# Loaded operands of 256-column matmuls begin 52 bytes behind their stream modulo 256, not 88

## The chip, the cores and the metric

One Trainium2 chip, one of its cores. The metric is the device time of one execution in microseconds; of the kernel before three runs are shown, and their median is 273.35 us (273.21 to 273.37).

## What is computed

One decoder layer on 256 tokens of width 1024, in float32. A hybrid mixer projects x with one combined matrix (1024 x 5120), makes an attention group, a gated linear recurrence (RG-LRU) and a gated short convolution of it, and projects their concatenation back (1536 x 1024); a layer norm follows, then cross-attention with 4 heads into 256 memory tokens, and a second layer norm. Cut to what matters:

```python
proj = x @ w_in                                  # (256, 1024) @ (1024, 5120)
q, k, v, g_att, x_lru, g_lru, sc_b, sc_c, sc_x, g_sc = split(proj, 10)
y = stack([moba_attention(q, k, v), rg_lru(causal_dwconv(x_lru)), sc_b * causal_dwconv(sc_c * sc_x)])
x = layer_norm(ALPHA * x + (group_rms_norm(y) * silu(gates)) @ w_out)
q, k, v = x @ wq, mem @ wk, mem @ wv             # 4 heads of 256
x = layer_norm(ALPHA * x + softmax(q @ k.T / 16) @ v @ wo)
```

## The kernel before

Every large product is made of three float32r products: each operand is split into a high part (an ACT copy, line 88) and a low part (a DVE subtraction, line 89), and TensorE adds high x high, high x low and low x high in one bank. The weights come in 42 chunks of 128 x 2048 numbers; `ORDER` (lines 40 to 55) is their order. SP loads a chunk into one of three `raw` buffers, ACT and DVE split it in two pieces into `whi` and `wlo` (four buffers each, pool `splp`), and TensorE reads these. The order of TensorE's work is that of the program, with small steps moved between the matmuls by the planner of the framework; chunks are split up to two ahead of the one in use.

TensorE takes two operands from SBUF in a matmul: one is loaded into the array ahead of time (a weight load, PEld in the profile), and the other streams through it. Each weight load here has 128 columns, 512 bytes in a partition, and the load for the next matmul goes on while the present one streams. There are two kinds of chunk:

- "Transposed" chunks (fourth entry of `ORDER` true; `proj_t`, lines 121 to 135): the weights are loaded and the activations stream, 256 columns or 1024 bytes each. These are the 16 chunks of the q, k, short-convolution and gate projections (the last two on tiles named `scc`, `scx`, `scb`, `gate`), the four of the cross-attention's keys (`km`) and the four of its queries (`xq`), 48 matmuls each. The first projection (`xlru`, line 194) works the same way with 96 matmuls.
- The others (`mm_n`, lines 140 to 148): the activations are loaded and the weights stream, 512 columns each, for the attention's values (`vb`), the mixer's output (`op`) and the memory's values (`vm`). The last projection (`ob`) uses this helper with 256 columns.

Where the operands begin in SBUF is set by hand. `at` (lines 70 to 76) gives a tile LINE = 64 numbers (256 bytes) more than it needs and returns it from a given number on. Weights that are loaded begin at AT_LOAD = 22 numbers (88 bytes), weights that stream in 512 columns at AT_STREAM = 7 (28 bytes), those of the last projection at 0. The buffers themselves begin at a multiple of 256 bytes, or 128 bytes past one (pool `con`, which holds x, the memory and their split parts; for tiles that meet these, HALF = 32 numbers is added). So in all 256-column matmuls of float32r numbers the loaded operand lies 88 bytes behind the streamed one modulo 256: the projections, the small gates of the recurrence (`early`, lines 270 to 289), the cross-attention's scores (`xs`, queries at HALF + AT_LOAD against keys at HALF) and values (`xo`), and `ob` (`oh` and `ol` at HALF + AT_LOAD). They are 24 x 48 + 96 + 24 + 48 + 48 + 192 = 1560 matmuls of about 2000. In the 512-column ones it is 228 bytes (`vb`, `vm`) or 100 (`op`). All later steps in a chunk are multiples of 256 bytes, so the difference stays through a chunk.

Of the kernel before, what the change touches and what calls it, by code (L numbers as in the profile page):

```python
# [26 lines left out]
XW = S + G  # L27


AT_LOAD, AT_STREAM, LINE, HALF = 22, 7, 64, 32  # L30
RAW, SPL, PIECES = 3, 4, 2


# [687 lines left out]
```

## Time and profile before

| | us |
|---|---|
| median of three runs | 273.35 |
| the profiled execution | 273.52 |
| its span, first to last instruction | 271.7 |
| PE busy in the span | 262.6 |
| DVE busy | 203.6 |
| ACT busy | 153.7 |

The profile has a page of sums and a trace that can be asked for more. PE is TensorE's matmuls, PEld its weight loads. The chain is the work that ended last, followed back from the end; its rows merge neighbours of one line and tile, so that time divided by count is the distance from one matmul's start to the next one's (the pitch). In a timeline row the second number is from the first start to the last end of the merged instructions, so a pitch is read there as the distance between starts of two rows, divided by the matmuls between them.

### The profile page before, as it was taken

To read this page: it belongs to the slowest core of one execution; us is meant where nothing else is said; L and a number is where in the kernel's file an instruction comes from. 1 tells how busy PE (TensorE), PEld (TensorE's weight loads), DVE (VectorE), ACT (ScalarE), POOL (GpSimd) and SP (SyncE) were. 2 spreads that over 40 slices of the span, in tenths; PEclk is the share of its full clock that TensorE was granted. 3 is DMA by queue.
4 is the path that set the end of the run, shared out by engine and by line. 5 is a ranking of instruction groups with operands and counts; after the bars stand their busy time and mean duration, and the time that the engine had idled before them with its cause. 6 is when DMAs were issued, how large, how long until landed. Compare 5 with 4: busy or idle time off the path is not lost.

```text
span 271.7 us, 4877 instructions
## 1 busy us (share of the span) xinstructions
PE 262.6 (97%) x2003; PEld 246.7 (91%) x2003; DVE 203.6 (75%) x279; ACT 153.7 (57%) x239; POOL 48.4 (18%) x67
## 2 busy tenths in 40 slices
PE   8999999999999999999999999999999999999990
PEld 5899998799999999999888889998899998899990
DVE  3889956699886998886897689957464759733735
ACT  4779599955995455746842344336554628623000
POOL 5582003006360979100000000000000000000000
PEclk9999999999999999999999999999999999999997
DMA  6994797244408647856675454687464440000012
GB/s 233 385 373 175 283 382 260 122 154 157 154 2 349 273 154 288 310 178 217 247 230 236 174 189 154 256 308 271 124 230 154 157 154 0 4 0 2 2 75 77
DMA packets 8118, 50.93 MB, mean 187 GB/s; under 512 B 912, under 2 KB 1312, under 8 KB 2464
## 3 DMA queue, kind: packets, MB, share of 16 engines
q1 hardware_dynamic: 8064, 50.60, 50.6%
q8 instruction: 15, 0.25, 0.3%
q14 instruction: 7, 0.06, 0.1%
q0 software_dynamic: 32, 0.03, 0.0%
HBM read 49.57 MB, written 1.05 MB: 186 GB/s over the span
## 4 chain that ended last, share of the span: by engine, by line
PE 92%; DMA 3%; DVE 2%; SPq 1%; ACT 1%; issue 0%; DVEq 0%
PE op L146 12%; PE gate L131 12%; PE vm L146 8%; PE xq L131 8%; PE ob L146 8%; PE km L131 8%; PE scb L131 4%; PE scc L131 4%; PE scx L131 4%; PE q L131 4%; PE vb L146 4%; PE k L131 4%; DMA raw_xw<-in_first 3%; PE xo L622 2%; PE xs L592 2%; PE xlru L194 2%
## 5 line engine op out<-in xcount | busy, mean ns | idle before, releaser
L89 DVE TENSOR_TENSOR wlo<-raw_w,whi 128x1024 fp32r<-128x1024 f32 x80 | 102.3, 1312 | 17.6 <-ACT whi L88 17.3
L88 ACT ACTIVATE whi<-raw_w 128x1024 fp32r<-128x1024 f32 x80 | 80.1, 1054 | 51.3 <-PE op L146 16.3
L146 PE MATMUL op<-whi,yh 128*128 128x512 f32 x64 | 16.7, 393 | 0.0
L146 PEld LDWEIGHTS op<-whi,yh 128*128 128x128 f32 x64 | 12.0, 189 | 2.6
L146 PE MATMUL op<-wlo,yh 128*128 128x512 f32 x48 | 13.0, 391 | 0.0
L131 PE MATMUL gate<-xh,wlo 128*128 128x256 f32 x96 | 12.8, 276 | 0.0
L131 PE MATMUL gate<-xh,whi 128*128 128x256 f32 x96 | 12.8, 276 | 0.0
L131 PE MATMUL gate<-xl,whi 128*128 128x256 f32 x96 | 12.8, 276 | 0.0
L501 DVE SCALAR_TENSOR_TENSOR xa<-op,rms,xa 128x512 f32<-128x512 f32 x12 | 8.8, 746 | 5.0 <-PE op L146 5.0
L131 PEld LDWEIGHTS gate<-xh,wlo 128*128 128x128 f32 x96 | 11.8, 188 | 0.0
L131 PEld LDWEIGHTS gate<-xh,whi 128*128 128x128 f32 x96 | 11.8, 188 | 0.0
L131 PEld LDWEIGHTS gate<-xl,whi 128*128 128x128 f32 x96 | 11.8, 188 | 0.0
L146 PEld LDWEIGHTS op<-wlo,yh 128*128 128x128 f32 x48 | 9.1, 189 | 2.0
L519 ACT ACTIVATE mvb<-mvb,eps_ln 128x1 f32<-128x1 f32 x2 | 0.6, 294 | 18.1 <-DVE mvb L518 18.1
L146 PE MATMUL ob<-whi,kml 128*128 128x256 f32 x64 | 10.2, 276 | 0.0
L146 PE MATMUL ob<-whi,kmh 128*128 128x256 f32 x64 | 10.1, 277 | 0.0
L146 PE MATMUL ob<-wlo,kmh 128*128 128x256 f32 x64 | 10.0, 276 | 0.0
L650 DVE SCALAR_TENSOR_TENSOR xa<-xa,ob 128x256 f32<-128x256 f32 (+1 forms) x7 | 3.2, 459 | 8.6 <-PE ob L146 8.4
L88 ACT ACTIVATE yh<-sg 128x512 fp32r<-128x512 f32 x6 | 3.8, 630 | 10.2 <-DVE sg L468 10.2
L131 PE MATMUL xq<-x1h,whi 128*128 128x256 f32 x64 | 9.3, 279 | 0.0
L146 PE MATMUL vm<-whi,mh 128*128 128x512 f32 x32 | 9.1, 399 | 0.0
L131 PE MATMUL xq<-x1l,whi 128*128 128x256 f32 x64 | 8.9, 277 | 0.0
(217 smaller groups left out, 638.0 us busy)
## 6 DMA issues: line engine op xcount, KB each, us to landing
raw_w<-in_w SPq DMA_DIRECT2D x40, 1024.0 KB, 4.8
lnv<-in_ln SPq DMA_DIRECT2D x2, 1024.0 KB, 8.1
raw_xw<-in_first SPq DMA_DIRECT2D x2, 768.0 KB, 8.4
xa<-in_x SPq DMA_DIRECT2D x1, 1024.0 KB, 6.8
raw_mem<-in_memt SPq DMA_DIRECT2D x1, 1024.0 KB, 4.8
raw_xw<-in_first SPq DMA_DIRECT2D x2, 384.0 KB, 6.1
raw_xw<-in_first SPq DMA_DIRECT2D x1, 512.0 KB, 4.1
out<-xa SPq DMA_DIRECT2D x2, 256.0 KB, 2.0
```

Of the source, the lines that this page charges most:

```text
L88: nc.scalar.activation(hi, src, AF.Copy)
L89: nc.vector.tensor_tensor(lo, src, hi.bitcast(F32), op=ALU.subtract)
L131: nc.tensor.matmul(ps[:, c], w[:, k, cs], a[:, k], start=n == 0, stop=n == 3 * KC - 1)
L146: nc.tensor.matmul(out, a[:, k0 + k, t * P:(t + 1) * P], part[w][:, k, c:c + out.shape[-1]], start=first and n == 0, stop=last and n == 11)
L194: nc.tensor.matmul(xlp[ct], w[:, k % 4, ct * P:(ct + 1) * P], x[:, k], start=k == 0 and m == 0, stop=k == 7 and m == 2)
L501: nc.vector.scalar_tensor_tensor(a, bk[t], rms[:, g, t:t + 1], a, op0=ALU.mult, op1=ALU.add)
L519: nc.scalar.activation(mv[:, 2:3], mv[:, 1:2], AF.Sqrt, bias=eps_ln)
L592: nc.tensor.matmul(ps[:, t], q[:, d, t * P:(t + 1) * P], k[:, 2 * h + d], start=n == 0, stop=n == 5)
L622: nc.tensor.matmul(po[:, d], v[:, m, c:c + P], p[:, m], start=n == 0, stop=n == 5)
L650: nc.vector.scalar_tensor_tensor(a, a, ALPHA, bank[:, :w], op0=ALU.mult, op1=ALU.add)
```

## The change

AT_LOAD, the place where loaded operands begin in their tiles, goes from 22 numbers to 13, from 88 bytes to 52. It is used for the transposed chunks and the first two (line 82), for the split gate weights of the recurrence (line 272), for `oh` and `ol` (line 509), for the memory's values `vmh` and `vml` (line 510) and for the queries `qh` and `ql` (line 582). No tile changes its size or its place, and no instruction, wait or transfer is added, removed or moved.

```diff
-AT_LOAD, AT_STREAM, LINE, HALF = 22, 7, 64, 32
+AT_LOAD, AT_STREAM, LINE, HALF = 13, 7, 64, 32
```

## Rows read from the trace of the kernel before

**Rows 1.** The page: busy time of TensorE's two parts, its granted clock in 40 slices.

```profile
PE 262.6 (97%) x2003; PEld 246.7 (91%) x2003; DVE 203.6 (75%) x279; ACT 153.7 (57%) x239; POOL 48.4 (18%) x67
PEclk9999999999999999999999999999999999999997
```

**Rows 2.** Chain that ended last, in order of time: start us, us, engine, tile, line.

```profile
13.25 4.93 PE xlru L194 x40
18.18 7.93 PE q L131 x68
...
43.06 11.04 PE vb L146 x48
...
62.72 5.60 PE scx L131 x48
...
96.23 32.64 PE gate L131 x288
...
129.16 33.24 PE op L146 x144
162.40 21.79 PE km L131 x192
184.19 1.75 PE x1t L548 x16
...
245.49 19.08 PE ob L146 x168
264.57 0.02 issue
264.59 0.43 DVE xa L650
```

**Rows 3.** Timeline of PE, ends of three long stretches: start us, us, instruction.

```profile
13.82 0.63 PE L194 MATMUL xlru<-xh,whi 128*128 128x256 f32 x4
...
27.82 0.28 PE L289 MATMUL gate<-xch,early 128*128 128x256 f32 x1
...
57.89 1.10 PE L131 MATMUL scc<-xl,whi 128*128 128x256 f32 x8
...
73.76 0.30 PE L331 MATMUL ss<-ones,thirds 128*128 128x1 bf16 x6
...
82.98 1.09 PE L131 MATMUL scx<-xl,whi 128*128 128x256 f32 x8
...
86.71 1.09 PE L131 MATMUL scx<-xh,wlo 128*128 128x256 f32 x8
...
217.25 1.09 PE L131 MATMUL xq<-x1l,whi 128*128 128x256 f32 x8
...
219.11 0.40 PE L592 MATMUL xs<-kmh,qh 128*128 128x256 f32 x2
```

**Rows 4.** Busy time by window: us, PE, PEld, DVE, ACT, POOL, PEclk, DMA share, GB/s.

```profile
57.89:72.82 14.93, 14.93 (x130) 14.93 (x129) 13.96 (x24) 9.79 (x28) 6.01 (x9) 1.00 0.37 123
82.98:86.71 3.73, 3.73 (x34) 3.73 (x33) 2.77 (x3) 1.09 (x3) 0.00 (x0) 1.00 0.97 406
75.76:79.39 3.63, 3.63 (x34) 3.63 (x33) 3.40 (x4) 3.63 (x6) 3.63 (x2) 1.00 0.02 5
96.06:127.80 31.74, 31.74 (x283) 31.74 (x281) 26.96 (x32) 18.75 (x24) 11.58 (x13) 1.00 0.65 235
```

**Rows 5.** Timeline of PE where `xo` and `ob` alternate: ends of 13 matmuls.

```profile
242.42 0.40 PE L622 MATMUL xo<-ptl,vmh 128*128 128x256 f32 x2
...
243.97 0.39 PE L622 MATMUL xo<-pth,vmh 128*128 128x256 f32 x2
```

**Rows 6.** DVE on `wlo`, 145 to 160 us (begins at 88), then 120 to 141 (28).

```profile
L89 DVE TENSOR_TENSOR wlo<-raw_w,whi x6: 1206/1216/1219, 146.5 to 159.3; 128x1024 fp32r<-128x1024 f32 x6
...
L89 DVE TENSOR_TENSOR wlo<-raw_w,whi x8: 1217/1222/1227, 119.1 to 138.7; 128x1024 fp32r<-128x1024 f32 x8
```

**Rows 7.** Waits: who waited for whom, us in total, times, longest.

```profile
ACT whi L88 <- PE scx L131: 2.8, 1, 2.8
```

## Prediction

> **What bounds the kernel now.** I read the busy times first: PE is busy for 262.6 of 271.7 us, and its granted clock is full in every slice but the last [rows 1], which is the level of 2.4 GHz. Next the chain in order of time, to see whether that busy time is also the path: from 13.25 to 264.57 us it is TensorE alone, matmul behind matmul [rows 2]. DVE takes over at 264.59 for the last layer norm, and ahead of 13.25 stand the first loads and splits. So each nanosecond of a matmul's pitch between those two times is a nanosecond of the kernel.
>
> Then I read the pitch, as time by count. One stretch of the chain has 288 matmuls of 256 columns in 32.64 us: 113.3 ns, which is 272 cycles at 2.4 GHz. Another has 48 of the same shape and the same offset in 5.60 us, which is 116.7 ns or 280 cycles; a third 68 in 7.93 us, 116.6 ns [rows 2]. So at one and the same offset there are two steady pitches, 3.33 ns or 8 cycles apart. The timeline shows long unbroken stretches at the slower one: 120 matmuls from 13.82 to 27.82 us (14.00 us, 116.7 ns each), 136 from 57.89 to 73.76 (15.87 us, 116.7 ns), 32 from 82.98 to 86.71 (3.73 us, 116.6 ns) and 16 from 217.25 to 219.11 (1.86 us, 116.3 ns) [rows 3].
>
> What picks the pitch is not another engine or the transfers. Two windows at 116.7 ns have a DMA share of 0.37 and of 0.97, two at 113.3 ns of 0.02 and of 0.65; POOL is busy throughout the window at 75.76 (113.3 ns) and idle throughout that at 82.98 (116.6 ns) [rows 4]. The pitch changes where the row of like matmuls is broken: behind the small gates, transposes or sums of another shape. I take it that each start sets how the weight load lies against the stream that runs beside it, that this repeats from matmul to matmul, and that the offset between the two operands says which repeating patterns there are. Behind a break the pitch can also be worse for a while: 13 matmuls where `xo` and `ob` alternate take 1.55 us, 119.2 ns each [rows 5].
>
> **The change, part by part.** It moves the start of the loaded operands, and that is all: nothing is issued, waited for or moved past a queue. There are three things to cost.
>
> *The writes of the splits.* ACT and DVE write the parts at another start. DVE's pieces take 1216 ns in the median where the tile begins at 88 bytes, and 1222 ns where it begins at 28 [rows 6], so the start does not show there. I cost it at nothing; what hides a few nanoseconds more is that the splits run ahead of TensorE.
>
> *Matmuls at 116.7 ns now.* Taken from the timeline in the way of [rows 3], 304 stand in the rows, and the like groups beside them (the rest of the `scc` and `scx` chunks, a few of `xq`) bring them to about 330. At the faster pitch they give back 330 x 3.33 ns = 1.10 us. Of the rest of the 1560, about 60 lie ahead of 13.82 us, most of them where splits set the time, some 110 are in the short transients behind breaks (at about 4 ns over 113.3 each, an estimate from the rows at 116 and 119 ns: 0.4 us in all), and about 1060 run at 113.3 ns, of which 648 stand in three rows of the chain (gate 288, km 192 at 113.5, ob 168 at 113.6 ns) [rows 2].
>
> *The price at 52 bytes.* No row has this offset with a long stretch, so it is bounded from both sides. From below: 113.3 ns is the least pitch in any stretch of 256 columns here. It is 17/16 of a cycle for each column, and by that same figure a matmul of 512 columns would take 226.7 ns; those of `vb` (at 228 bytes) take 11.04 us / 48 = 230.0 ns and those of `op` (at 100) 33.24 / 144 = 230.8 with their restart [rows 2]. No offset in this trace beats 17/16, so I take it as the floor. A lower end is the 109.4 ns of the 128-column transposes (1.75 us / 16) [rows 2], which load as many columns each: 3.9 ns less for 1500 matmuls. From above: the slower pitch, 116.7 ns, or far out the 119.2 of a transient [rows 5].
>
> I take the floor, since it is the value nearest to most rows: of the long stretches, some 1060 matmuls are on it and 330 are not, and a move by 36 bytes does away with the particular pattern that holds these 330. The sum: 273.52 us of the profiled execution less 1.10 is 272.42, and as that execution is 0.17 us above the median of the runs, 272.25 against 273.35; I say 272.2. The transients stay at their 0.4 us, because the breaks stay. What comes next behind a faster TensorE: in the window of the `scc`, `scx` and `scb` chunks DVE is busy for 13.96 of 14.93 us [rows 4], so its splits have 6% to spare for 3% of speed. One ACT split there waits 2.8 us for TensorE to free its buffer [rows 7]; such a wait shrinks as TensorE gets ahead. At the end nothing else is late before 264.57 us. If the cover fails in that stretch, half of its 0.45 us is lost.
>
> **A rule that speaks against it.** The two pitches at one offset, with all other engines different or idle, are what I have on how load and stream act on each other [rows 2 to 4]. The Trainium skill (SBUF — State Buffer, "Who interferes with whom") gives TensorE two independent read ports, one for the moving operand and one for weight loads, and says that it never waits on anyone; by that rule the offset is of no account and the time stays at 273.35 us. The trace neither proves nor excludes it, since it has no two long stretches that differ in the offset alone; it stands below as a rival. The skill's page on TensorE (TensorE: Matmul & The Clock Gate, "Wait — 56ns, not 53.3ns?") gives a warm gap of N/2.4 + 2.5 ns, 109.2 for 256 columns; the rows here have 113.3 and 116.7 instead.
>
> **The rivals.**
>
> *It settles on 280 cycles.* At 52 bytes the repeating pattern with 8 cycles more may be the one that holds everywhere. What speaks for it: the 288 matmuls of 512 columns pay 3.3 ns over 17/16 throughout [rows 2], and their offsets, 228 and 100, leave 4 modulo 16 as 52 does, while 88 leaves 8. If a fine position like that decides, the whole kernel goes to 116.7 ns. Against it: those have another length and another stream. Its price: 1060 x 3.33 = 3.53 us, 276.9. If each stretch falls to either pitch by chance, half of 1390 matmuls are at 116.7 ns instead of 330: 365 x 3.33 = 1.2 us more, 274.6. It decides from the point at which more than 330 of these 1390 run at 280 cycles.
>
> *Nothing that counts.* The pattern is set by how the queue restarts after a break, not by where the operands lie, or the offset doesn't bear on the load's reads at all, so that the change does not do what its words say. For it: both pitches exist at 88. Against it: the pitch holds for a hundred matmuls on end, which looks like a position that repeats. The time: 273.35, within 0.5.
>
> *Below the floor.* At 52 bytes load and stream don't meet, and the pitch comes down to the 109.4 ns of the transposes: 1500 x 3.9 = 5.9 us, and 1.5 for what now lies above 113.3 ns, 266. Against it: no full-rate stretch is under 17/16, at three offsets and two lengths.
>
> *Above 280 cycles.* All at the transient's 119.2 ns: 1060 x 5.9 + 330 x 2.5 = 7.1 us, 280.4.
>
> **How the numbers follow.** The forecast has a chance of 0.43, below the floor 0.05: faster 0.48. Nothing that counts 0.18. The 116.7 ns for all or by chance 0.28, worse 0.06: slower 0.34. What a measurement of this kernel can tell from no change is about 0.2%, 0.55 us. The forecast's own range is 271.8 (transients gone too) to 272.7 (only half of the stretches at 116.7 ns gone). The 8 in 10 leave out what is below the floor and what is above 280 cycles, 0.11 together, and a little at both edges: 271.7 to 277.0.
>
> **What would show it.** Right: `q`, `scx` and `scb` in the chain at 5.44 us for 48 instead of 5.60, the gates' 288 still at 32.64, `op` and `vb` unmoved, and TensorE still the chain from its first to its last matmul. The first rival: `gate` 288 at 33.6 us and `km` 192 at 22.4. Below the floor: `gate` at 31.5. What makes me wrong is that a pattern at 88 says little about the one at 52: no row has that offset, and the sign hangs on it.

## The result and the profile after

The changed kernel took 274.76 us (median of 273.48, 274.5, 275.03 and 275.37) against 273.28 us for the kernel before: a ratio of 1.0051 [1.0034, 1.0067]. In a second comparison it took 274.1 us (ten runs, 272.39 to 275.71) against 273.7, 1.0011 [0.9985, 1.0037]. So it is slower, by something between nothing and 0.7%, and it spreads over 3.3 us where the kernel before spreads over 1.7 (272.85 to 274.56). I had forecast 272.2.

The profiled execution of the changed kernel took 273.48 us, the lowest of the first four. This is its granted clock in 40 slices, as in [rows 1]:

```profile
PEclk9999999999999999999999999999999999999998
```

And its chain of waits in order of time (start us, us, engine, tile, line), to be held against [rows 2]:

```profile
2.57 7.81 DMA raw_xw<-in_first
...
13.31 4.83 PE xlru L194 x40
18.14 7.71 PE q L131 x68
25.85 1.81 PE k L131 x16
...
27.78 3.36 PE q L131 x28
...
56.90 5.66 PE scc L131 x48
62.56 5.44 PE scx L131 x48
68.00 5.44 PE scb L131 x48
...
79.98 1.75 PE pt L404 x16
81.73 5.76 PE scx L131 x48
87.50 2.75 PE ya L417 x32
90.25 5.68 PE scb L131 x48
95.93 32.64 PE gate L131 x288
...
128.86 33.24 PE op L146 x144
```

Four rows of the kernel before that stand beside these and not in [rows 2]:

```profile
26.11 1.87 PE k L131 x16
...
28.10 3.19 PE q L131 x28
...
56.92 5.80 PE scc L131 x48
...
68.32 5.60 PE scb L131 x48
```

The clock is still full in every slice but the last, and TensorE is still the chain. Below I use one number for it, the *TensorE chain*: from the first of the 40 `xlru` matmuls to the start of the last matmul (0.29 us ahead of the end of the last PE row). Before it is 264.57 - 13.25 - 0.29 = 251.03 us, here 250.82. A chain that is given as a number is this one. A row behind a break includes the *restart*, the longer distance to its first matmul; the pitch that a stretch holds behind that is called *settled*. By stretch, the part up to the first small gate went from 14.73 us (4.93 + 7.93 + 1.87) to 14.35; the three chunks `scc`, `scx`, `scb` from 17.00 to 16.54. Both settled at 113.3 ns, 0.84 us less together. But `q` x28 behind the small gate went from 3.19 us to 3.36, 3.36 / 28 = 120.0 ns, and from that gate to `vb` the stretch is 0.29 us longer. The second `scx` went from 116.7 to 120.0 ns (+0.16 us), the stretch from `x1t` to `ob` grew by 0.14, and 0.04 lies in smaller pieces. Of 0.84 us gained, 0.21 is left.

That would make the kernel 0.1% faster. The median is slower, so other executions may have another chain. I took two more profiles of the same kernel. The chain of the first of them (274.87 us; columns as above):

```profile
2.58 8.08 DMA raw_xw<-in_first
...
13.58 4.81 PE xlru L194 x40
...
80.23 1.83 PE pt L404 x16
82.06 5.48 PE scx L131 x48
...
90.29 5.85 PE scb L131 x48
96.14 33.92 PE gate L131 x288
```

The same instructions, and yet the 288 gate matmuls take 33.92 us, 117.8 ns each, where [rows 2] and the first profile after have 32.64 (113.3). The second `scx` is at 113.3 ns (5.48 with its restart), `scb` at 117.8. This chain is 252.04 us, that of the third profile 252.00: a whole microsecond over the kernel before.

The timeline of PE shows this pitch too. After, first profile, then second (start us, us, instruction):

```profile
95.77 1.07 PE L131 MATMUL gate<-xh,whi 128*128 128x256 f32 x8
...
100.30 0.96 PE L131 MATMUL gate<-xh,wlo 128*128 128x256 f32 x7
```

```profile
95.98 1.10 PE L131 MATMUL gate<-xh,whi 128*128 128x256 f32 x8
...
100.69 0.52 PE L131 MATMUL gate<-xh,wlo 128*128 128x256 f32 x3
```

Forty matmuls lie between the two rows: 4.53 us, 113.3 ns, and 4.71 us, 117.8 ns. The busy time by window over 30 us of the gates, first profile and second (us, PE, PEld, DVE, ACT, POOL, PEclk, DMA share, GB/s):

```profile
96.30:126.30 30.00, 30.00 (x267) 30.00 (x266) 25.86 (x30) 17.71 (x22) 12.12 (x13) 1.00 0.65 244
```

```profile
96.30:126.30 30.00, 30.00 (x257) 30.00 (x256) 25.85 (x30) 17.86 (x23) 12.15 (x13) 1.00 0.68 242
```

Clock, transfers and every other engine are alike; TensorE gets through 267 matmuls in the one and 257 in the other.

One thing more has to be taken out before times are compared: the first load. In this profile it took 8.08 us, in that above 7.81, and over the 15 profiled executions of the layer, of nine kernels, 7.52 to 8.53. It moves the start of `xlru` and with that the end, one for one: time less start less TensorE chain is 9.2 to 9.35 us in all of them (273.52 - 13.25 - 251.03 = 9.24 before; 274.87 - 13.58 - 252.04 = 9.25 here). So a kernel is read best by its TensorE chain, and a single time says little below 1 us.

### The profile page after: what moved, and what is told of

It is laid out like the page before. It is cut to its first block, busy times and chain, and to the rows that moved or that the text cites. A ratio compares the mean times of both kernels' runs of the same rounds, so it can differ in the third digit from the quotient of the medians.

```text
span 271.6 us, 4877 instructions
## 1 busy us (share of the span) xinstructions
PE 262.9 (97%) x2003; PEld 247.0 (91%) x2003; DVE 203.8 (75%) x279; ACT 153.7 (57%) x239; POOL 47.9 (18%) x67
## 3 DMA queue, kind: packets, MB, share of 16 engines
HBM read 49.57 MB, written 1.05 MB: 186 GB/s over the span
## 4 chain that ended last, share of the span: by engine, by line
PE 93%; DMA 3%; DVE 1%; SPq 1%; ACT 1%; issue 0%; DVEq 0%
PE op L146 12%; PE gate L131 12%; PE vm L146 8%; PE xq L131 8%; PE ob L146 8%; PE km L131 8%; PE scx L131 4%; PE scc L131 4%; PE scb L131 4%; PE q L131 4%; PE vb L146 4%; PE k L131 4%; DMA raw_xw<-in_first 3%; PE xlru L194 2%; PE xo L622 2%; PE xs L592 2%
## 5 line engine op out<-in xcount | busy, mean ns | idle before, releaser
L89 DVE TENSOR_TENSOR wlo<-raw_w,whi 128x1024 fp32r<-128x1024 f32 x80 | 98.8, 1268 | 18.0 <-ACT whi L88 17.8
```

Of the source, the lines that this page charges most:

```text
L89: nc.vector.tensor_tensor(lo, src, hi.bitcast(F32), op=ALU.subtract)
```

## The experiments

Three theories stood at the start. That the offset sets which repeating patterns there are, as in the forecast, but that at 52 bytes some are dearer than 116.7 ns. That the offset is of no account and breaks alone set the pitch. And that the weight chunks gain as forecast and the small matmuls (`early`, `xs`, `xo`, `ob`), which the same constant moves, lose it again.

### The same kernel twice more

No edit.

> The changed kernel once more, unaltered, for a profile of another execution. Theory A (two repeating patterns at 52 bytes, 113.3 and 120.0 ns, and which stretch falls on which differs from execution to execution): the span is longer or shorter than the first profile's 271.6 us by 6.67 ns for each matmul of 256 columns more or fewer at 120 ns, within 0.2 us; the time lies between 272.5 and 276 us. Theory B (the executions differ elsewhere, at the start or in waits for splits): the same stretches at 120 ns as in the first profile, and the difference stands in gaps between stretches or ahead of 13 us.

> A third profile of the changed kernel. Theory A: again span = 271.6 us plus 6.67 ns for each matmul at 120 ns more than in the first profile, and at least one long stretch on another pattern than in the other two. Theory B: the same stretches at 120 ns each time.

Measured: the two profiles above, with chains of 252.04 and 252.00 us. What follows: one program has at least two chains 1.2 us apart, and the difference lies between the transposes `pt` and the end of the gates. The dear pitch is 117.8 ns and not the 120.0 that I expected.

### The chunks alone

```diff
-AT_LOAD, AT_STREAM, LINE, HALF = 13, 7, 64, 32
+AT_CHUNK, AT_LOAD, AT_STREAM, LINE, HALF = 13, 22, 7, 64, 32
...
-        o = AT_LOAD if j < 2 or ORDER[j][3] else 0 if ORDER[j][0] == "o" else AT_STREAM
+        o = AT_CHUNK if j < 2 or ORDER[j][3] else 0 if ORDER[j][0] == "o" else AT_STREAM
```

> Does the change for the weight chunks alone (52 bytes there; the recurrence's gates, the scores, the values and the last projection stay at 88). Theory A: the 1248 matmuls of the chunks are most of it, so stretches at 120 ns show as in the whole change, and the time is 273.5 to 275.5 us, spread over 1 us or more from run to run. If the small matmuls made the loss (theory C), the time is that of the kernel before, 273.0 to 273.4, with little spread.

Measured: 274.71 us (274.11 to 276.23), ratio 1.0042 [1.0024, 1.006]; chain 251.88, gates 33.92. What follows: the loss is in the chunks. The third theory falls.

### All offsets, in a stream by itself

A kernel that computes nothing of the layer. For each of 64 offsets (4 bytes apart) there are three streams of 32 matmuls of 256 columns; ahead of each stands one of three breaks: four transposes, four matmuls of 512 columns, or two sums of one column.

```python
for o in range(64):
    for kind, brk in (("t", tr), ("w", wide), ("s", sums)):
        ...
        nc.tensor.matmul(ps, w[:, o + k * 256 + c * P:o + k * 256 + c * P + P], s[:, k * 256:(k + 1) * 256], ...)
```

> Leaves the whole computation out: only streams of 32 matmuls of 256 columns, at each of the 64 offsets of the loaded operand (0 to 252 bytes behind the stream), each offset three times, behind 4 transposes (t), 4 matmuls of 512 columns (w) and 6 of one column (s). Tile names: at_, two letters for the offset in numbers of 4 bytes (8 x first + second, a = 0), and t, w or s. Theory A: at 22 numbers (cg) the settled pitch is 113.3 or 116.7 ns, at 13 (bf) 113.3 or 120.0; other offsets have their own pairs, none under 113.3, some with 113.3 behind all three breaks. Rival (the offset doesn't matter, the break alone does): one and the same pitch behind a kind of break at all 64 offsets.

Measured: the chain of waits has a row for each stream, the restart included. These are 52 bytes (`bf`) and 88 (`cg`) behind transposes and behind sums:

```profile
180.08 3.68 PE at_bft L58 x32
...
188.47 3.77 PE at_bfs L58 x32
...
296.22 3.67 PE at_cgt L58 x32
...
304.60 3.94 PE at_cgs L58 x32
```

From the starts of the last 17 matmuls of each stream (ns between two):

| offset, bytes | transposes | 512 columns | sums |
|---|---|---|---|
| 52 | 113.4 | 113.3 | 113.4 |
| 88 | 113.3 | 113.4 | 120.0 |
| 64 | 113.3 | 113.3 | 117.8 |
| 76 | 120.0 | 113.3 | 113.3 |
| 168 | 120.0 | 113.3 | 113.3 |
| 8 | 115.6 | 115.5 | 115.6 |
| 20 | 120.0 | 120.0 | 120.0 |
| 28 | 116.7 | 116.6 | 116.7 |

At 52 bytes I had expected 113.3 and 120.0, at 88 113.3 and 116.7; the streams have 113.3 alone, and 113.3 and 120.0. None of the 64 goes below 113.3; 52 is the only one at it behind all three; most lie between 116.6 and 120, a few up to 123. What follows: the offset does decide, and the second theory falls. The Trainium skill (SBUF — State Buffer, "Who interferes with whom") says that TensorE never waits on anyone; here, with no other engine at work, the pitch depends on where the two operands lie by up to 10 ns, so that rule doesn't cover load against stream. And taken by itself this table would choose 52 bytes, the offset that loses in the kernel. So 32 matmuls behind three breaks aren't the kernel.

### Many breaks at five offsets

The same stream, with 55 breaks at each of five offsets: 24 pairs of bf16 matmuls of 1 to 47 columns, 1 to 16 transposes, 1 to 8 times four half-width matmuls as in `ya`, and 1 to 7 matmuls at another start of the stream. It too leaves out the layer.

> Leaves the whole computation out: streams of 32 matmuls of 256 columns with the loaded operand 52 (first), 88 (second), 64 (third), 76 (fourth) or 168 bytes (fifth) behind, each behind 55 different breaks: two matmuls of 1 to 47 columns (short), 1 to 16 transposes (turned), 1 to 8 pairs of half-width matmuls (halves, the form of line 417), 1 to 7 matmuls whose stream lies 128 bytes further (moved). Theory A: each offset has a small set of repeating pitches and the break picks one; at 52 bytes 113.3, 117.8 and 120.0 ns all occur, at 88 bytes 113.3, 116.7 and 120.0; behind the half-width pairs 52 bytes gives 117.8 in some of eight and 113.3 in others. Rival (at 52 bytes 113.3 is the only pattern and what the kernel shows there comes from its other engines): 113.3 to 113.5 behind all 55 breaks.

Measured, streams out of 55 at each settled pitch (last 18 distances; the very first stream, 147.5 ns in the mean, is left out at 52):

| offset | 113.3 | 116.7 | 117.8 | 120.0 | mean |
|---|---|---|---|---|---|
| 52 | 45 | 0 | 3 | 6 | 114.3 |
| 88 | 23 | 29 | 0 | 3 | 115.5 |
| 64 | 17 | 0 | 38 | 0 | 116.4 |
| 76 | 53 | 0 | 0 | 2 | 113.6 |
| 168 | 30 | 0 | 0 | 25 | 116.4 |

Three rows of its chain, behind half-width matmuls at 52 bytes:

```profile
211.94 3.84 PE first_halves L62 x32
...
218.54 3.97 PE first_halves L62 x32
...
251.72 3.84 PE second_short L62 x32
```

The first two differ by 0.13 us for 32 matmuls with the restart in both: settled, 113.3 and 117.8 ns. The third is 88 bytes behind a short break, settled at 116.7. What follows: each offset has its own few pitches. 88 has 113.3 and 116.7 and now and then 120; 52 has 113.3, 117.8 and 120 and never 116.7. The kernel's 33.92 us for 288 is the 117.8 of 52 bytes, and in this stream too it comes up behind half-width matmuls, 2 times in 8, of which one (the row at 218.54) is behind 32 of them. `ya`, ahead of `scb`, is 32 of this form.

### A break ahead of the gates

Six matmuls of one column between the second `scb` and the gates, to see whether a break ends the pattern.

```diff
+    with tc.issue_after(last[0].ins):
+        ps = pp.tile([P, 2], F32, tag="ps", name="fence")
+        for i in range(6):
+            nc.tensor.matmul(ps[:, :1], still, ones1, start=i == 0, stop=i == 5)
```

> The changed kernel with six matmuls of one column set between the last scb matmul and the first of the 288 gate matmuls. Theory A (a stretch keeps the pattern that its start gives it, and behind such a break 52 bytes settles at 113.3 to 113.4): the 288 take 32.6 to 32.7 us in every execution instead of 33.92 in two of three; the break costs 0.25 to 0.35 us; median 273.2 to 274.0. Rival (the pitch of the gates follows from what runs beside them): 33.9 us as before, and the time 274.3 to 275.

> The kernel with six one-column matmuls ahead of the gates once more, for an execution in which the second scx falls on 113.3 ns. Theory A: scb then stands at 5.85 us (117.8 ns), as in the two profiles of the change that had it so, and the gates behind the break at 32.8 all the same. Rival (the pitch of the gates follows from what runs beside them): scb 5.85 and the gates at 33.9.

Measured: 274.23 us (273.54 to 275.39), ratio 1.0026 [1.0008, 1.0043]. That is above the 273.2 to 274.0 that I expected, although neither profile has the gates at 33.9 us: their chains are 251.07 and 251.01, level with the 251.03 of the kernel before, and their `xlru` starts late, at 14.03 and 13.87. So the median doesn't show the gain, and what follows rests on the profiles. The first profile happened to have `scb` at 113.3 already and tells nothing of the break but its price, 0.14 us and a restart of 0.13. The second, of the same kernel, had the case. Its chain:

```profile
80.52 1.78 PE pt L406 x16
82.30 5.48 PE scx L131 x48
...
90.53 5.85 PE scb L131 x48
96.38 0.14 PE fence L477 x6
96.53 32.79 PE gate L131 x288
```

`scb` ran at 117.8 ns, and behind 0.14 us of other work the same matmuls at the same offset ran at 113.3 (32.79 with the restart). What follows: the pitch is drawn at a break and was kept until the next one, for 288 matmuls in the profiles with 33.92. Without the break they inherit what `scb` drew.

### What draws it

In the profile of the second execution `pt` took 1.83 us, in the first 1.75. These are the 16 transposes of the attention's probabilities, and the fifth needs POOL's second normalization (line 387). The timeline of POOL in the kernel before:

```profile
75.39 4.73 POOL L387 TENSOR_TENSOR p<-p,l 128x1024 f32<-128x1024 f32 x2 [1.92 <-DVE l L385]
```

and of the second profile after, with PE's transposes in its own timeline:

```profile
75.74 4.73 POOL L387 TENSOR_TENSOR p<-p,l 128x1024 f32<-128x1024 f32 x2 [1.92 <-DVE l L385]
...
80.06 1.99 PE L404 MATMUL pt<-ident,p 128*128 128x128 f32 x16
```

POOL ends at 80.12 and 80.47. The fifth transpose would begin four pitches of 109.4 ns (0.44 us) behind the first: at 80.06 + 0.44 = 80.50 here, and at 80.30 + 0.44 = 80.74 before. TensorE has got ahead by 0.46 us in `scc`, `scx` and `scb` and by 0.08 to 0.1 in front of them, while POOL, behind a chain of its own, is no earlier against the start of `xlru` (62.14 us behind it before, 62.16 here). The *slack*, from POOL's end to the time at which the fifth transpose would begin, fell from 0.62 to 0.03 us. The profiles so far of the kernel before and of those with 52 bytes in all chunks, by that slack:

| profile | slack | `pt` x16 | 2nd `scx` | `scb` | gates | TensorE chain | time |
|---|---|---|---|---|---|---|---|
| before | 0.62 | 1.75 | 5.60 | 5.67 | 32.64 | 251.03 | 273.52 |
| before, again | 0.54 | 1.75 | 5.60 | 5.67 | 32.64 | 251.03 | 273.94 |
| break ahead of gates | 0.17 | 1.75 | 5.76 | 5.68 | 32.77 | 251.07 | 274.35 |
| after | 0.11 | 1.75 | 5.76 | 5.68 | 32.64 | 250.82 | 273.48 |
| after, third | 0.09 | 1.77 | 5.50 | 5.86 | 33.92 | 252.00 | 275.03 |
| break, second | 0.08 | 1.78 | 5.48 | 5.85 | 32.79 | 251.01 | 274.13 |
| after, second | 0.03 | 1.83 | 5.48 | 5.85 | 33.92 | 252.04 | 274.87 |
| chunks alone | 0.03 | 1.84 | 5.50 | 5.85 | 33.92 | 251.88 | 274.76 |

Below a slack of 0.1 us the transposes stall for 0.02 to 0.09 us. Wherever they stall, `scx`, at 52 bytes, falls to 113.3 instead of 120.0 ns, and `scb`, behind `ya`, to 117.8 instead of 113.3. A stall of 20 ns goes with a loss of 1.2 us, nearly all of it behind `ya`. But stall and `scx` go together in this table, so which of the two carries it takes runs that part them.

### Taking the wait away

The changed kernel with the transposes in another order: all of one half of the heads first, so that POOL's second normalization is needed 0.44 us later.

```diff
-        for kc in range(t + 1):
-            for a in range(2):
+        for a in range(2):
+            for kc in range(t + 1):
```

> The changed kernel with the 16 transposes ahead of the second scx in another order (both column halves of the heads of the first half, then of the second), so that POOL's second normalization is needed 0.44 us later. Theory A2 (the 16 transposes have 0.07 us or less in hand at 52 bytes; where they stall for POOL, the second scx falls on another pattern, and through the half-width matmuls behind it scb and the 288 gate matmuls fall on 117.8 ns): no stall (16 transposes in 1.75 us), scx 5.76, scb 5.68, gates 32.64 in every execution, median 273.1 to 273.6, level with that of before or 0.3 us under it, and no execution over 274.8. Rival (the stall goes along with the pattern but doesn't set it; gates fall on 117.8 ns by chance in two of three executions): gates at 33.92 as often as not, median 274.1 to 274.8.

> The changed kernel with the transposes reordered, a second profile. Theory A2: no stall, scx 5.76, gates 32.64, chain of TensorE 250.8 us as in the first; what its time differs by is the landing of the first load. Rival (chance): transposes at 1.75 all the same, but scx at 5.48 and gates at 33.92.

> A third profile of the same kernel. Theory A2: as above, chain 250.8 us. Rival: gates at 33.92 without a stall in this or the second.

Measured: 273.8 us (272.73 to 275.22), ratio 1.0016 [0.9998, 1.0033]; the expected median, 273.1 to 273.6, missed. In all three profiles `pt` 1.75, the second `scx` 5.76, gates 32.64: the stall doesn't come up, nor do the 117.8 ns there. If chance put the gates on 117.8 in two of three executions, three profiles without would come up once in 27. Two chains are 250.80 and 250.81 us. The third is 251.34, by something else. Its start, with the same columns:

```profile
18.97 8.01 PE q L131 x68
...
32.76 4.32 PE k L131 x36
```

Here the 68 of `q` are at 117.8 ns and the 36 of `k` at 120.0; in every other profile at 52 bytes they are at 113.3 (7.71) and 114.4 (4.12). So the first long stretch too can draw another pattern, here behind the 40 of `xlru` (4.98 us instead of 4.81 to 4.83). What draws it isn't shown: the waits of TensorE for the splits in that stage are much the same in the third profile after (0.8 us for `wlo` and 0.5 for `whi`, against 0.9 and 0.4 here), and there `q` is at 113.3. My expectation that no execution would be above 274.8 missed: 275.22 came up, and 251.34 + 9.25 and the latest start in a profile, 14.03, make only 274.6. That execution had a later start or a dearer chain that no profile caught. Later starts can't be excluded: the kernel before has an execution of 274.56 us, which at its chain of 251.03 would start at 14.28. It stays open.

### The break in place of the wait

The changed kernel with its old order of transposes and the same six matmuls of one column, between these and the second `scx`.

> The changed kernel with six matmuls of one column between the 16 transposes and the second scx. In the kernel of streams 52 bytes settles at 113.3 ns behind every such break. Theory A2, its second link (the pattern of the second scx, through the half-width matmuls behind it, sets that of scb and the gates: scx at 113.3 gave gates at 117.8 in three profiles, scx at 120.0 gave gates at 113.3 in two): scx 5.44 to 5.50, and, although nothing is saved on the gates, scb 5.85 and gates 33.92 in each execution; chain of TensorE 252.2 us or more, median 274.3 to 275.2. Rival (it is the stall itself, or chance, that puts the gates on 117.8): gates at 32.64, chain 250.8 to 251.0, median 273.3 to 273.9.

Measured: 274.93 us (274.52 to 275.95), ratio 1.0054 [1.0035, 1.0073], as expected; the lowest of the eight is above the median of the reordered kernel, 273.8. Its chain:

```profile
80.14 1.75 PE pt L406 x16
81.89 0.13 PE fence L412 x6
82.02 5.57 PE scx L131 x48
...
90.34 5.86 PE scb L131 x48
96.19 33.91 PE gate L131 x288
```

No stall (`pt` 1.75), `scx` at 113.3 ns (5.57 with the restart), and `scb` and gates at 117.8 all the same. What follows: the stall is only one way to put `scx` on another pattern. The state in which `scx` runs is handed through the 32 matmuls of `ya` to `scb` and from there to the gates. The cheaper `scx` saves 0.19 us against the first profile after (0.28 without the break, in the second), and `scb` and gates pay 1.45 us for it.

### The offset where it gains, and nowhere else

52 bytes in the chunks 0, 1, 2 and 8 to 10 alone (`xlru`, the first of `q`, the first `scc`, `scx` and `scb`), 88 elsewhere.

```diff
-AT_LOAD, AT_STREAM, LINE, HALF = 13, 7, 64, 32
+AT_FIRST, AT_LOAD, AT_STREAM, LINE, HALF = 13, 22, 7, 64, 32
...
+        o = AT_FIRST if j in (0, 1, 2, 8, 9, 10) else AT_LOAD if ORDER[j][3] else 0 if ORDER[j][0] == "o" else AT_STREAM
```

> The kernel before with 52 bytes in those chunks alone that ran at 113.3 ns in all three profiles of the change and at 116.7 in that of before (the two of xlru, the first of q, and the first scc, scx and scb); 88 bytes elsewhere. Theory A: 40 + 48 + 136 matmuls give back 3.33 ns each, 0.75 us, and up to 0.1 more if the next chunks stay on 113.3: the chain has q 68 at 7.71 to 7.80, scx and scb at 5.44, the gates at 32.64, and the median is 272.5 to 273.0 where that of before is 273.4 to 273.7. If a change of offset from chunk to chunk throws a stretch onto another pattern, q or scc behind the switch stands at 116.7 or 120, and the gain is under 0.4 us.

Measured: 273.24 us (272.68 to 274.42) against 273.47, ratio 0.9993 [0.9979, 1.0007]. The median missed the 272.5 to 273.0 that I expected. The chain is 250.60: 0.43 us less and not 0.75. Two of its rows:

```profile
72.99 1.05 PE pt L404 x8
74.04 5.60 PE scc L131 x48
```

The second `scc`, still at 88, went from 5.46 to 5.60 (116.7 ns), and the 16 transposes behind it took 1.91. What ended their idle time (us, times):

```profile
  POOL p L387: 0.2, 1
```

What follows: the cover that I had not costed, seen by name. Behind that stall `scx` and gates are as before, 5.60 and 32.64. But the eight transposes ahead of the second `scc` stalled too (1.05 us instead of 0.94), and there the pitch at 88 bytes went from 113.3 to 116.7. So a stall may pick another pattern at 88 as well; since the chunk's offset also changes from 52 to 88 just there, this run doesn't tell the two apart.

Then the same with the chunk of the second `scc` (11) at 52 too, and the transposes in the new order.

```diff
+        o = AT_FIRST if j in (0, 1, 2, 8, 9, 10, 11) else AT_LOAD if ORDER[j][3] else 0 if ORDER[j][0] == "o" else AT_STREAM
...
-        for kc in range(t + 1):
-            for a in range(2):
+        for a in range(2):
+            for kc in range(t + 1):
```

> The kernel before with 52 bytes in the chunks of xlru, the first of q, the first scc, scx and scb and the second scc, 88 elsewhere, and the transposes in the order of the run before. Theory A2: xlru 40 at 4.83, q 68 at 7.71, scc 5.66, scx and scb 5.44, second scc 5.47, transposes 1.75, second scx 5.60, scb 5.67, gates 32.64: 0.80 to 0.86 us off the chain from the first of the 40 xlru matmuls to the first step of DVE behind the last matmul, which was 251.34 us in both profiles of before; median 272.4 to 272.9. Rival: transposes in another order put the second scx or the gates on a slower pattern, and the chain is 251.2 us or more.

Measured: 273.13 us (272.45 to 273.33) against 273.46, ratio 0.9983 [0.9972, 0.9995]. Its chain:

```profile
74.66 5.46 PE scc L131 x48
80.12 1.75 PE pt L404 x16
81.87 5.60 PE scx L131 x48
...
95.89 32.64 PE gate L131 x288
```

The chain is 250.18 us, 0.85 under the kernel before, as expected of it; the profiled time, 273.19, has a late start (13.76). The median is 0.33 us better, less than the chain, and better than both kernels. The difference of 0.5 us between chain and median isn't accounted for by a run; the expected median (272.4 to 272.9) missed.

### Another offset for all

```diff
-AT_LOAD, AT_STREAM, LINE, HALF = 13, 7, 64, 32
+AT_LOAD, AT_STREAM, LINE, HALF = 19, 7, 64, 32
```

> The same change with 19 numbers, 76 bytes, in place of 13. In the kernel of streams 76 bytes settled at 113.3 ns behind 53 of 55 breaks (all short ones, half-width pairs and moved streams), 120.0 behind two of the transposes. Theory A (the break and the offset pick the pattern, so what a stream shows behind a kind of break holds in the kernel): xlru, q, the first scc, scx and scb and the gates at 113.3 (q 68 at 7.71, scx and scb 48 at 5.44, gates 288 at 32.64), a loss at most behind the transposes (second scc and scx, 120 ns); what stands above 113.3 is 0.5 to 1.1 us instead of 1.77; median 0.5 to 1.2 us under that of before. Rival (patterns in the kernel don't follow those of the streams): some other long stretch, the gates above all, at 117 to 120 and the time at or above that of before.

Measured: 273.4 us (272.79 to 274.28) against 273.43, ratio 0.9999 [0.9984, 1.0014]; chain 250.68. The chain is 0.35 us under the kernel before, but the gain of 0.5 to 1.2 us in the median that I expected didn't come. The second `scc` and `scx` are at 120.0 ns behind transposes (5.76 and 5.75), nearly all else at 113.3, gates 32.64. What follows: at 76 bytes no 117.8 came up, here or in the 55 streams, and with it no loss, though the slack at its transposes is 0.10 us and `pt` 1.76.

### The kernel before, once more

> The kernel before once more, for a second profile. Theory A: its stretches at 88 bytes fall on the same pitches as in the first profile to within one or two stretches, with 116.7 as the other one; span 271.2 to 272.8 us. If it is as unsteady as the changed kernel, the gates' 288 matmuls stand at another pitch than 113.3.

Measured: a chain of 251.03 us, as in the first profile, in stretch after stretch, and 273.94 us because the first load took 8.16 us instead of 7.77. What follows: at 88 bytes with 0.5 us of slack the two profiles have one chain. That every execution has it isn't shown.

## Why the prediction was wrong

*What bounds the kernel.* Right. TensorE stays the chain in all profiles, and a nanosecond of pitch is a nanosecond of time: time less start less chain is 9.2 to 9.35 us everywhere.

*Two repeating pitches set by offset and break, not by other engines.* Right in that offset and break set them, and now shown, though there are more than two: the sweep has nothing else at work and still has them, the windows over the gates are alike but for the count of matmuls, and a break of 0.14 us changed 117.8 into 113.3. Another engine bears on it only at the break, by a stall.

*The writes of the splits at nothing.* Nothing speaks against it: the chain is TensorE, and `op` is at 33.24 us in both.

*The matmuls at 116.7 ns, 1.10 us.* Half right. `xlru`, `q`, the first `k`, and the first `scc`, `scx` and `scb` came down as forecast, 0.84 us. The second `scx` didn't: 5.60 became 5.76 or 5.48, and neither helped.

*The price at 52 bytes: "I take the floor".* This step failed. That 113.3 ns is the floor held at all 64 offsets. But I reasoned from how many matmuls at 88 bytes are on it to a pitch at 52, as if an offset had one pitch with some exceptions. It has a set of them, and that of 52 holds 117.8 and 120.0, both dearer than 116.7. The mis-sized terms: the price behind the breaks, taken as unchanged, grew by 0.29 us behind the small gates (0.17 of it in 28 matmuls of `q` that stood at 113.3 and went to 120.0) and by 0.14 behind the cross-attention's; the second `scx` paid 0.16 more in the first profile; and 336 matmuls that stood at 113.3 went to 117.8 in two of three profiled executions, 1.28 us in the gates and 0.18 in `scb`.

*"What comes next behind a faster TensorE".* This failed too, and it set off the dearer half. I looked at DVE and ACT for cover in that stretch, not at POOL, which [rows 4] shows busy throughout the window at 75.76. (That nothing is late at the end of the kernel held: 9.2 to 9.35 us everywhere.) TensorE's lead of 0.5 us in front of the transposes brought it to POOL's end with 0.03 to 0.11 us to spare instead of 0.62. The stall itself, 0.02 to 0.09 us, is less than the half of 0.45 that I allowed for it. Its price was the pattern behind it.

*The rivals.* The time fell to the first, and the price I gave for "either pitch by chance", 274.6, is near the median of 274.76, by luck: it was worked out from other matmuls at another pitch. Its mechanism is half right: not the 280 cycles that I named (52 bytes never shows 116.7) but 282.7, and not chance stretch by stretch but one state handed from `scx` through `ya` to 336 matmuls. "Nothing that counts" falls with the sweep. "Below the floor" and "all above 280 cycles" didn't come up. The gap that the Trainium skill (TensorE: Matmul & The Clock Gate, "Wait — 56ns, not 53.3ns?") gives, by estimate 109.2 ns for 256 columns, is reached at none of 64 offsets here, where the least is 113.3.

*What stays open.* Why the array has these patterns, and why 52 bytes has 117.8 where 88 has 116.7. Why transposes that stall put `scx` on 113.3 and those that don't on 120.0. How often each chain comes up: three profiles of the changed kernel can't say, and the two comparisons (1.0051 and 1.0011) don't agree. The execution at 275.22 us with the transposes reordered. And what else is in the medians: in all seven further kernels that were timed against the kernel before, the median came out 0.16 to 0.72 us worse against it than the chain of the first profile did (`best` -0.33 against -0.85, the break ahead of the gates +0.76 against +0.04). So some of the loss of the changed kernel, too, can lie ahead of the chain, in when the first load lands, or in chains that no profile caught; no run tells which.

## What to carry to other kernels

Read a change of layout by the pitch of each stretch (time by count in the chain), not by the median, and in more than one profile: here a stretch of like matmuls kept the pitch that it drew at the last break, so that one program can have chains 1.2 us apart. An offset that is best in a stream by itself needn't be so behind the breaks of the kernel; move it stretch by stretch, where the pitch is above the least one, and leave alone what is already there. When a stage gets faster, work out the slack of every producer at the next point where the engines meet, the one with the least work too: here a stall of 20 ns went with a loss sixty times itself.

## What the runs showed of the hardware

- Matmuls of 256 float32r columns with a weight load of 128 behind each settled at 113.3 to 123.3 ns in a stream by itself, by the offset of the two operands modulo 256 bytes and by the break ahead, and at 113.3, 116.7, 117.8 or 120.0 ns (272 to 288 cycles at 2.4 GHz) in the long stretches of the kernels; none of 64 offsets goes below 113.3, and no other engine is needed for it.
- The pitch was kept from break to break (288 matmuls at 117.8 ns) and can be drawn again by six matmuls of one column (0.13 to 0.14 us and as much for the restart).
- With 52 bytes in all chunks, a stall of 0.02 us or more in front of `scx` went with another pattern in four profiles of four, and five without one, three of them with the wait taken away, kept theirs. What is drawn outlives 32 half-width matmuls: without a stall, the added break ahead of `scx` gave the same 117.8 ns behind `ya`, in one profile.
- The same first load took 7.52 to 8.53 us in 15 executions of nine kernels (7.81 to 8.27 in three of one kernel) and moved the end by as much. Two executions of the same kernel before differ by 0.42 us in time and by nothing in the TensorE chain.
